# First group of a recurrent encoder layer on one core: weights in contiguous rows, two blocks per input piece, a constant as warm-up operand

## The chip, the cores and the metric

The kernel runs on one core of a Trainium2 chip. The metric is the device time of one execution in microseconds. The kernel before was timed three times. Besides, one execution was recorded by the hardware profiler; all times of single instructions are from that one.

## The reference, cut to what matters

One layer, 1024 positions by 1024 channels, all float32. The input product makes six blocks of 1024 columns; a gated linear recurrence (A) and a multi-scale pooling (B) work on two of them, the others are gates.

```python
h = x @ w_in + b_in                       # 1024 x 1024  @  1024 x 6144
xa, za, xb, zb, ga, gb = split(h)
ya = RG_LRU(causal_conv4(xa)) * silu(za)
yb = MultiScalePool(xb) * silu(zb)
y  = (sigmoid(ga) * (ya @ w_proj_a) + sigmoid(gb) * (yb @ w_proj_b)) @ w_out + b_out
out = LayerNorm(alpha * x + y)
```

## The kernel before, in words

**Products.** A float32 operand is split into a rounded high part (a CAST on ACT, names ending in h) and a low part (a TENSOR_TENSOR subtraction on DVE, names ending in l). Each product is three passes into one PSUM bank: high by high, weight high by input low, weight low by input high (`passes`, line 449). Two output blocks of 128 columns, one from each half of a section, are made together as a 2x2 block product with seven instead of eight multiplications (Winograd's form). So there are seven inputs `X[1..7]` and for every group seven weights. The names are: `x13` (products 1 and 3), `x2` and `xb` plain quarters of the input; `x57` and `x64` sums of quarters, from the raw sums `t13` and `t24`; `wa` (products 1, 2), `wb` (7, 5), `wc` (6, 3) and `wd` (4) for the weights, from the raw `ra` and `rb`. A product of one group is 12 matmuls of 512 columns: four pieces of 128 in depth, three passes each.

**Order.** PE's order is the program's. The first group, "G0" (gate columns 0 and 4), is made from plain quarters, 8 products of 4 pieces, while the input comes in (bank names `ps_s`, lines 953 to 1098). Group A0 follows (line 1125 on): product 1 (`a_A`), 2 (`e_A`), 5 (`f_A`, copied out by ACT as `m5`), 7 (`c_A`, copied out as `m7`), 3 (`f_A` again). Then it runs mixed with the next group, G1: products 1 and 2 of G1 (`a_G`, `e_G`), 6 of A0 (`a_A`), 7 of G1 (`c_G`), 6 of G1 (`a_G`), 4 of A0 (`c_A`), and so on through 24 groups, the two projections and the output product.

**The planner.** Nothing is issued directly. `Plan.add` (line 179) records every instruction with its data dependences; `Plan.order` (line 252) goes through them as a list scheduler, with a cost for each kind of instruction, a due time that follows from PE's ideal times (line 260) and the costs behind, and picks on ACT, DVE, SP and POOL the ready task that is due first, holding back when one that is due earlier becomes ready soon. `emit` writes them out in that order, so that every instruction stands at line 388. On the chip each engine then works strictly in the written order: an instruction that waits holds all that stand behind it on its engine.

**The start.** DVE clears a tile `warm` (line 955), and PE does WARM = 6 products of zeros with it. ACT issues the transfers of the first quarter of the two weight blocks (`w0r`, `dma_w0`), SP those of the input (`xr`) and the later weights. The weight block lies in HBM as 128 partitions x 8 pieces x 128 columns. A quarter of depth takes pieces q and q + 4 of it, so a transfer of one quarter has two rows of 512 bytes per partition, that of two quarters two rows of 1 KB. The first quarter of block 0 comes as two transfers of 64 KB. In the loop at line 1082 the first 512 x 128 input piece is used in two halves of 256 columns with block 0; the second piece (`kh == h == 1`) is used whole with block 0, and only then block 1 is split and used with both pieces.

**The end.** SP loads the weights of the output product (`wor`, in two transfers for each of its seven steps), the rows of the layer norm, and fills seven eighths of the output with a bias row (line 1429), to which POOL later adds.

Of the kernel before, what the change touches and what calls it, by code (L numbers as in the profile page):

```python
# [11 lines left out]
F32 = mybir.dt.float32  # L12
F32R = mybir.dt.float32r
AF = mybir.ActivationFunctionType
ALU = mybir.AluOpType

P = 128
# [3 lines left out]
H = 512  # L21
# [2 lines left out]
EPS = 1e-5  # L24
WINDOWS = (2, 4, 8, 16)
PAD = 16
WARM = 6
NW = 10
NR = 4
NWORK = 10  # L30
# [367 lines left out]


@with_exitstack  # L400
def layer_kernel(ctx: ExitStack, tc: tile.TileContext, xq, x, w_in, par, wg, w_pool, wpa, wpb, w_out, rows, out):
    nc = Plan(tc)

    def pool(name, bufs, space=None):
# [13 lines left out]
    def xt(name, dt=F32R, shape=(P, 2, H)):  # L418
        return xpool.tile(list(shape), dt, tag="x", name=name)

    def wt(name, dt=F32R, shape=(P, 2, H)):
        return wpool.tile(list(shape), dt, tag="w", name=name)
# [4 lines left out]
    def kt(name, dt=F32):  # L427
        return kpool.tile([P, S], dt, tag="k", name=name)

    def et(name):  # L430
        return epool.tile([P, H], F32, tag="e", name=name)

    def bank(name):
        return psum.tile([P, H], F32, tag="ps", name=name)
# [4 lines left out]
    out = Ref(result, as_strided(Ref.base, [S, D], [D, 1]))  # L439
    HALF = [slice(0, H), slice(H, S)]  # L440
    V, A = nc.vector, nc.scalar
# [8 lines left out]
    def split(raw, hi, lo):  # L450
        A.copy(hi, raw)
        V.tensor_tensor(lo, raw, hi.bitcast(F32), ALU.subtract)

    def passes(ps, w, m, first, last):
        (wh, wl), (mh, ml) = w, m
        for i, (a, b) in enumerate(((wh, mh), (wh, ml), (wl, mh))):
            nc.tensor.matmul(ps, a, b, start=first and i == 0, stop=last and i == 2, skip_group_check=True)
# [9 lines left out]
    KQ = 4  # L467
# [127 lines left out]
    order = [("G", 0)]  # L595
# [4 lines left out]
    def blocks_of(kind, c):  # L600
        if kind == "A":
            return XA + c, ZA + c
        if kind == "B":
            return XB + c, ZB + c
        sec = GA if c < 4 else GB
        return sec + c % 4, sec + c % 4 + 4
# [297 lines left out]
    def b_pool(g):  # L904
# [15 lines left out]
        if g == 1:  # L920
# [5 lines left out]
    sp, m, nl, y, z, z2, acc = (const.tile([P, 8], F32, name=n)  # L926
                                for n in ("sp", "sp_m", "sp_nl", "sp_y", "sp_z", "sp_z2", "sp_acc"))
# [22 lines left out]


    begin = ctx.enter_context(ExitStack())
    pass
    warm = kt("warm", F32R)[:, :H]
    V.memset(warm.bitcast(F32), 0.0)
    psw = bank("ps_warm")
    for i in range(WARM):
        nc.tensor.matmul(psw, warm[:, 0:P], warm, start=True, stop=True)
    first = blocks_of(*order[0])
    wr, wh, wl = [[f(f"{t}{n}") for n in range(2)] for t, f in  # L960
                  (("w0r", lambda n: wt(n, F32)), ("w0h", wt), ("w0l", wt))]

    xr = [[kt(f"xr{q}_{i}", F32) for i in range(2)] for q in range(KQ)]
    x13 = [[xt(f"x13{t}{q}") for t in "hl"] for q in range(KQ)]
    x2 = [xt(f"x2_{q}") for q in range(KQ)]
    xb = [xt(f"xb_{q}") for q in range(KQ)]

    def w0_part(t, n, a, b):
        return t[n].rearrange("p h (k m) -> p h k m", m=P)[:, :, a:b, :]

    def dma_w0(n, a, b, h=slice(0, 2)):

        (A if a == 0 else nc.sync).dma_start(w0_part(wr, n, a, b)[:, h], w_in[first[n]].rearrange("p (h k) m -> p h k m", h=2)[:, h, a:b, :])

    def split_w0(n, a, b, h=slice(0, 2)):
        split(*(w0_part(t, n, a, b)[:, h] for t in (wr, wh, wl)))

    def dma_x(q, i, sl=slice(0, S)):
        nc.sync.dma_start(xr[q][i][:, sl], xq[q, i][:, sl])


    def quarter(q, kh, h):
        if kh == h:
            return x13[q][0][:, kh, :], x13[q][1][:, kh, :]
        t = x2[q] if kh else xb[q]
        return t[:, 0, :], t[:, 1, :]
# [3 lines left out]
    def split_x(q, kh, h, sl=slice(0, H)):  # L990
        i, p = raws[kh, h]
        split(xr[q][i][:, HALF[p]][:, sl], *(t[:, sl] for t in quarter(q, kh, h)))

    ps0 = [[bank(f"ps_s{n}_{h}") for h in range(2)] for n in range(2)]

    def mm0(q, kh, h, n, cs=slice(0, H)):
        sl = slice(q * P, (q + 1) * P)
        passes(ps0[n][h][:, cs], (wh[n][:, kh, sl], wl[n][:, kh, sl]), tuple(t[:, cs] for t in quarter(q, kh, h)),
               q == 0 and kh == h and cs.start == 0, q == KQ - 1 and kh != h)


    PARTS = [slice(0, H // 2), slice(H // 2, H)]
    dma_w0(0, 0, 1, slice(0, 1))
    with nc.within(-2 * SOON):
        for sl in PARTS:
            dma_x(0, 0, sl)
    dma_w0(0, 0, 1, slice(1, 2))
    dma_w0(1, 0, 1)
    dma_x(0, 0, HALF[1])
    dma_x(0, 1, HALF[0])  # L1010
# [14 lines left out]
    t13, t24 = [None] * KQ, [None] * KQ  # L1025
# [15 lines left out]

    def sum57(q):
        t13[q] = xt(f"t13_{q}", F32)
        r = xr[q][0].rearrange("p (i s) -> p i s", i=2)
        V.tensor_tensor(t13[q], r, xr[q][1][:, HALF[0]].unsqueeze(1).to_broadcast((P, 2, H)), ALU.subtract)

# [19 lines left out]
    def parts(q, n=0):  # L1066
        r = xr[q][0].rearrange("p (i s) -> p i s", i=2)
        todo = [(r, *x13[q])] + [(xr[q][raws[p][0]][:, HALF[raws[p][1]]], *quarter(q, *p)) for p in ((0, 1), (1, 0))]
        for raw, t, u in todo[n:]:
            hi(raw, t)  # L1070
        for raw, t, u in todo[n:]:
            lo(raw, t, u)
        for kh, h in ((0, 0), (1, 1), (0, 1), (1, 0)):
            for n in range(2):
                mm0(q, kh, h, n)

    def each(f, qs, *a):
        for q in qs:
            f(q, *a)

    split_w0(0, 0, 1, slice(0, 1))
    for kh, h in ((0, 0), (1, 1), (0, 1), (1, 0)):
        if kh == h == 1:
            split_w0(0, 0, 1, slice(1, 2))
        for sl in PARTS if kh == h == 0 else (slice(0, H),):
            split_x(0, kh, h, sl)
            mm0(0, kh, h, 0, sl)
        if kh == h == 1:
            split_w0(1, 0, 1)
            mm0(0, 0, 0, 1)  # L1090
        if kh or h:
            mm0(0, kh, h, 1)
    for i in range(2):
        split_x(1, i, i)
        split_w0(i, 1, 2)
# [3 lines left out]
    w = weights_steps(1)  # L1099
    lower, upper = (0, 1), (2, 3)  # L1100
    each(sum57, lower)
    parts(2)
    each(hi57, lower)
    each(lo57, lower)
    parts(3)
    hi(w.ra, w.pair("wa", (1, 2))[0])
    each(sum57, upper)
    lo(w.ra, *w.tiles["wa"])
    w.sums75(wt("sb_A0", F32))
# [247 lines left out]
    for i, (n, j) in enumerate(steps):  # L1357
# [7 lines left out]
        if j == 1:  # L1365
            a, c, m1, um = [[None] * KQ for _ in range(4)]
        X_, W_ = ([(hi_[:, k, :], lo_[:, k, :]) for hi_, lo_ in ops[i][o:o + 2] for k in range(2)] for o in (0, 2))
        for g in range(KQ):
# [5 lines left out]
            for q in range(KQ):  # L1374
                sl = slice(q * P, (q + 1) * P)
# [10 lines left out]
            if (n, j) in DONE:  # L1386
                d, h = DONE[n, j]
                d += g
                if j == 3:
                    t, u = ps, et(f"c12_{n}{g}") if n == "b" else None  # L1390
                else:
                    t = u = m1[g] if j == 2 else um[g][:, HALF[h]]
# [12 lines left out]
            if (n, j, g) in CASTS:  # L1405
                k = CASTS.index((n, j, g))
# [89 lines left out]
    a, c = ([None] * KQ for _ in range(2))  # L1496
# [89 lines left out]
```

## Time and profile before

| quantity | value |
|---|---|
| median of 3 runs | 740.57 us (740.27 to 740.96) |
| profiled execution, its own time | 740.07 us |
| its span in the trace | 738.3 us |
| PE busy | 729.5 us, 99% of the span |
| DVE / ACT / POOL busy | 600.8 / 459.0 / 67.9 us |
| moved by DMA | 158.98 MB, mean 215 GB/s |

The span is from the first to the last instruction in the trace; the rest of the execution's time, 1.8 us, lies around it. PE works without a pause from the first microseconds to about 7 us before the end. In the views a row is start, duration, engine, line, operation, output <- inputs, shapes. A matmul's duration reaches to its modelled end; the step from one matmul's start to the next is what a matmul costs in the stream. The views leave out the numbers in the names: `m_A<-f_A` is `m5_A0<-f_A0`, `t<-t,xr` is a sum `t24`, `ps_s` is any of the four banks of G0.

### The profile page before, as it was taken

To read this page: it belongs to the slowest core of one execution; us is meant where nothing else is said; L and a number is where in the kernel's file an instruction comes from. 1 tells how busy PE (TensorE), PEld (TensorE's weight loads), DVE (VectorE), ACT (ScalarE), POOL (GpSimd) and SP (SyncE) were. 2 spreads that over 40 slices of the span, in tenths; PEclk is the share of its full clock that TensorE was granted. 3 is DMA by queue.
4 is the path that set the end of the run, shared out by engine and by line. 5 is a ranking of instruction groups with operands and counts; after the bars stand their busy time and mean duration, and the time that the engine had idled before them with its cause. 6 is when DMAs were issued, how large, how long until landed. Compare 5 with 4: busy or idle time off the path is not lost.

```text
span 738.3 us, 8785 instructions
## 1 busy us (share of the span) xinstructions
PE 729.5 (99%) x3249; PEld 599.4 (81%) x3249; DVE 600.8 (81%) x741; ACT 459.0 (62%) x587; POOL 67.9 (9%) x119
## 2 busy tenths in 40 slices
PE   9999999999999999999999999999999999999996
PEld 7887888888787878788888888888888888888885
DVE  7999796969696878977986768879948786999686
ACT  7686959686877868688844445447553545315473
POOL 0171011111101111100011100100000000000021
PEclk9999999999999999999999999999999999999999
DMA  9247979588988989842187954999679996758748
GB/s 320 111 142 198 264 180 279 135 240 224 303 161 217 328 206 282 219 113 91 54 204 154 212 114 158 278 315 331 235 241 303 311 333 234 267 201 232 196 80 149
DMA packets 64227, 158.98 MB, mean 215 GB/s; under 512 B 4340, under 2 KB 8308, under 8 KB 64120
## 3 DMA queue, kind: packets, MB, share of 16 engines
q1 hardware_dynamic: 43512, 106.26, 41.4%
q0 software_dynamic: 20112, 51.91, 33.6%
q8 instruction: 25, 0.41, 0.2%
q10 hardware_dynamic: 560, 0.26, 0.1%
q14 instruction: 18, 0.15, 0.1%
HBM read 137.43 MB, written 77.07 MB: 291 GB/s over the span
## 4 chain that ended last, share of the span: by engine, by line
PE 99%; DVE 1%; DVEq 0%; issue 0%
PE a_A L388 11%; PE a_B L388 11%; PE a_G L388 11%; PE oa L388 6%; PE pa_a L388 6%; PE pa_b L388 6%; PE c_B L388 6%; PE c_A L388 6%; PE c_G L388 5%; PE ps_s L388 3%; PE oc L388 3%; PE pc_b L388 3%; PE pc_a L388 3%; PE ps_pool L388 3%; PE e_B L388 3%; PE e_A L388 3%
## 5 line engine op out<-in xcount | busy, mean ns | idle before, releaser
L388 ACT ACT_TABLE_LOAD x38 | 48.8, 1283 | 3.0 <-issue 2.3
L388 DVE TENSOR_TENSOR i<-i,xc 128x1024 f32<-128x1024 f32 x8 | 9.8, 1225 | 26.9 <-ACT i L388 26.9
L388 DVE SCALAR_TENSOR_TENSOR xc<-xp,par_sb,xc 128x1023 f32<-128x1023 f32 (+2 forms) x24 | 30.7, 1281 | 0.5
L388 PE MATMUL pa_a<-oh,oh 128*128 128x512 f32 x64 | 24.9, 389 | 0.0
L388 PE MATMUL pa_a<-ol,oh 128*128 128x512 f32 x64 | 24.9, 389 | 0.0
L388 PE MATMUL pa_a<-oh,ol 128*128 128x512 f32 x64 | 24.9, 389 | 0.0
L388 PE MATMUL pa_b<-oh,oh 128*128 128x512 f32 x64 | 24.9, 389 | 0.0
L388 PE MATMUL pa_b<-ol,oh 128*128 128x512 f32 x64 | 24.9, 389 | 0.0
L388 PE MATMUL pa_b<-oh,ol 128*128 128x512 f32 x64 | 24.9, 389 | 0.0
L388 ACT ACTIVATE zb<-zb,par_sb 128x1024 f32<-128x1024 f32 (+1 forms) x16 | 15.0, 938 | 14.2 <-DVE zb L388 14.1
L388 ACT ACTIVATE r<-ps_g,par_sb 64x512 f32<-64x512 f32 x32 | 21.9, 683 | 2.1 <-DVE rb_B L388 0.8
L388 ACT ACTIVATE i<-ps_g,par_sb 64x512 f32<-64x512 f32 x32 | 21.9, 684 | 1.9 <-DVE r L388 1.4
L388 PE MATMUL c_A<-x64h,wd_A 128*128 128x512 f32 x64 | 21.0, 389 | 0.0
L388 PE MATMUL c_B<-x64h,wd_B 128*128 128x512 f32 x64 | 21.0, 389 | 0.0
L388 POOL DMA_DIRECT2D out<-y x7 | 8.5, 1210 | 130.0 <-ACT sd L388 117.4
L388 PE MATMUL ps_pool<-mixh,wp 128*128 128x512 f32 x64 | 20.3, 389 | 0.0
L388 PE MATMUL e_A<-x,wah_A 128*128 128x512 f32 x64 | 19.7, 389 | 0.0
L388 PE MATMUL e_B<-x,wah_B 128*128 128x512 f32 x64 | 19.7, 389 | 0.0
L388 POOL COPY paced<-pace 128x1 f32<-128x1 f32 x17 | 6.4, 376 | 130.9 <-ACT pace L388 130.9
L388 PE MATMUL c_G<-x64h,wd_G 128*128 128x512 f32 x56 | 18.4, 389 | 0.0
L388 DVE TENSOR_TENSOR_SCAN r<-a,i 128x1024 f32<-128x1024 f32 x8 | 18.3, 2284 | 0.1
L388 PE MATMUL e_G<-x,wah_G 128*128 128x512 f32 x56 | 17.2, 389 | 0.0
(521 smaller groups left out, 2534.5 us busy)
## 6 DMA issues: line engine op xcount, KB each, us to landing
sg<-sg SPq DMA_DIRECT2D x16, 512.0 KB, 4.3
ra_A<-in_w_in SPq DMA_DIRECT2D x8, 512.0 KB, 7.1
rb_A<-in_w_in SPq DMA_DIRECT2D x8, 512.0 KB, 7.5
xb<-bias SPq DMA_DIRECT2D x4, 1024.0 KB, 12.8
ya<-r SPq DMA_DIRECT2D x8, 512.0 KB, 5.7
xb<-in_x POOLq DMA_DIRECT2D x4, 1024.0 KB, 8.8
ra_B<-in_w_in SPq DMA_DIRECT2D x8, 512.0 KB, 4.3
rb_B<-in_w_in SPq DMA_DIRECT2D x8, 512.0 KB, 6.6
```

Of the source, the lines that this page charges most:

```text
L388: getattr(getattr(nc, t.op[0]), t.op[1])(*a, **k)
```

## The change

The host gives the two blocks of the first group once more as an array `w0`, laid out [block, partition, quarter, half, column], and the tiles `w0r`, `w0h` and `w0l` get the same layout. A quarter is then one row of 1 KB per partition, two quarters are one of 2 KB. The first quarter of each block is one transfer of 128 KB on ACT's queue (two in all where there were three). The warm-up's tile and its clearing are gone: PE multiplies a constant zero, read with step 0, WARM = 8 times. Both blocks are used on each piece of the first quarter in turn, and the second piece is also used in two halves with block 0. `sum57(0)` is done in two halves. Nothing else in the program's text changes.

```diff
-WARM = 6
+WARM = 8
...
-    warm = kt("warm", F32R)[:, :H]
-    V.memset(warm.bitcast(F32), 0.0)
+    warm = tc.nc.const_aps.tensor(0.0, [P, H]).bitcast(F32R)
...
-    wr, wh, wl = [[f(f"{t}{n}") for n in range(2)] for t, f in
-                  (("w0r", lambda n: wt(n, F32)), ("w0h", wt), ("w0l", wt))]
+    wr, wh, wl = [[wt(f"{t}{n}", dt, (P, KQ, 2, P)) for n in range(2)] for t, dt in
+                  (("w0r", F32), ("w0h", F32R), ("w0l", F32R))]
...
+    def dma_w0(n, a, b):
+        (A if a == 0 else nc.sync).dma_start(wr[n][:, a:b], w0[n][:, a:b])
+    def split_w0(n, a, b):
+        split(*(t[n][:, a:b] for t in (wr, wh, wl)))
...
-    dma_w0(0, 0, 1, slice(0, 1))
+    dma_w0(0, 0, 1)
     with nc.within(-2 * SOON):
         for sl in PARTS:
             dma_x(0, 0, sl)
-    dma_w0(0, 0, 1, slice(1, 2))
     dma_w0(1, 0, 1)
...
+        if q == 0:
+            for i in range(2):
+                V.tensor_tensor(t13[q][:, i, :], xr[q][0][:, HALF[i]], xr[q][1][:, HALF[0]], ALU.subtract)
+            return
...
-    split_w0(0, 0, 1, slice(0, 1))
     for kh, h in ((0, 0), (1, 1), (0, 1), (1, 0)):
-        if kh == h == 1:
-            split_w0(0, 0, 1, slice(1, 2))
-        for sl in PARTS if kh == h == 0 else (slice(0, H),):
-            split_x(0, kh, h, sl)
-            mm0(0, kh, h, 0, sl)
-        if kh == h == 1:
-            split_w0(1, 0, 1)
-            mm0(0, 0, 0, 1)
-        if kh or h:
-            mm0(0, kh, h, 1)
+        for n in range(2):
+            if kh == h == 0:
+                split_w0(n, 0, 1)
+            for sl in PARTS if kh == h and n == 0 else (slice(0, H),):
+                if n == 0:
+                    split_x(0, kh, h, sl)
+                mm0(0, kh, h, n, sl)
...
+        "w0": np.ascontiguousarray(w_blocks[[32, 36]].reshape(2, P, 2, 4, P).transpose(0, 1, 3, 2, 4)),
```

The planner orders the whole program anew from these tasks, so the written order also differs in places that the diff does not name. Here the rows keep the numbers in the names; the number after the last underscore only counts tiles.

ACT at the end of group A0's weights, before: `wch_A0` is the last weight of A0, `wah_G1` the first high weight of G1, `m5` and `m7` the copies of PE's products 5 and 7.

```order
L388 COPY m1_A0_370<-a_A0_347 128x512
L388 CAST wch_A0_380<-ra_A0_126 128x1024
L388 ACT_TABLE_LOAD
L388 ACTIVATE sp_y_399<-sp_m_377 128x8
L388 CAST wah_G1_401<-ra_G1_183 128x1024
L388 COPY m5_A0_430<-f_A0_392 128x512
L388 ACT_TABLE_LOAD
L388 ACTIVATE sg32_4_467<-ps_s1_0_178,par_sb_163 128x512
L388 ACTIVATE sg32_4_467<-ps_s1_1_186,par_sb_163 128x512
L388 COPY m7_A0_485<-c_A0_427 128x512
```

And ACT at the same place now.

```order
L388 COPY m1_A0_371<-a_A0_346 128x512
L388 CAST wch_A0_389<-ra_A0_125 128x1024
L388 ACT_TABLE_LOAD
L388 ACTIVATE sp_y_408<-sp_m_386 128x8
L388 COPY m5_A0_419<-f_A0_391 128x512
L388 CAST wah_G1_434<-ra_G1_193 128x1024
L388 COPY m7_A0_460<-c_A0_417 128x512
L388 ACT_TABLE_LOAD
L388 ACTIVATE sg32_4_490<-ps_s1_0_165,par_sb_170 128x512
```

`wah_G1` stood ahead of `m5_A0`, which reads a product of PE; now it stands behind it, and `m7_A0` is ahead of the gate's activations.

DVE where it makes G1's weights 7, 5, 6 and 3 (`wbl`, `wcl`), now:

```order
L388 TENSOR_TENSOR wd_G1_557<-rb_G1_236,wd_G1_557 128x512
L388 TENSOR_TENSOR rb_G1_236<-rb_G1_236 128x512
L388 TENSOR_TENSOR rb_G1_236<-ra_G1_193,rb_G1_236 128x512
L388 TENSOR_TENSOR ra_G1_193<-rb_G1_236,ra_G1_193 128x512
L388 TENSOR_TENSOR sg32_1_584<-e_G1_525,m1_G1_533 128x512
L388 TENSOR_TENSOR wbl_G1_588<-rb_G1_236,wbh_G1_581 128x1024
L388 TENSOR_TENSOR ra_G1_193<-ra_G1_193 128x512
L388 SCALAR_TENSOR_TENSOR xp0_395<-f_A0_391,par_sb_170,u2_A0_586 128x512
L388 TENSOR_TENSOR z0_605<-a_A0_346,m5_A0_419 128x512
L388 TENSOR_TENSOR wcl_G1_610<-ra_G1_193,wch_G1_601 128x1024
```

Between `wal_G1` and these rows stand the same 14 instructions of DVE as before, the sums `t24` and the low parts `x64l`; behind the second `ra_G1`, `xp0` stands where `wd_A0` stood.

PE's first rows, before:

```order
L388 MATMUL ps_warm_104<-warm_85 128x512 x6
L388 MATMUL ps_s0_0_150<-x13h0_142,w0h0_145 128x256
L388 MATMUL ps_s0_0_150<-x13l0_147,w0h0_145 128x256
L388 MATMUL ps_s0_0_150<-x13h0_142,w0l0_152 128x256
L388 MATMUL ps_s0_0_150<-x13h0_142,w0h0_145 128x256
L388 MATMUL ps_s0_0_150<-x13l0_147,w0h0_145 128x256
L388 MATMUL ps_s0_0_150<-x13h0_142,w0l0_152 128x256
L388 MATMUL ps_s0_1_168<-x13h0_142,w0h0_145 128x512
L388 MATMUL ps_s0_1_168<-x13l0_147,w0h0_145 128x512
L388 MATMUL ps_s0_1_168<-x13h0_142,w0l0_152 128x512
```

And now, `ps_s0` and `w0h0` being block 0, `ps_s1` and `w0h1` block 1:

```order
L388 MATMUL ps_warm_85<-const-float32-0.0 128x512 x8
L388 MATMUL ps_s0_0_151<-x13h0_141,w0h0_144 128x256
L388 MATMUL ps_s0_0_151<-x13l0_146,w0h0_144 128x256
L388 MATMUL ps_s0_0_151<-x13h0_141,w0l0_149 128x256
L388 MATMUL ps_s0_0_151<-x13h0_141,w0h0_144 128x256
L388 MATMUL ps_s0_0_151<-x13l0_146,w0h0_144 128x256
L388 MATMUL ps_s0_0_151<-x13h0_141,w0l0_149 128x256
L388 MATMUL ps_s1_0_165<-x13h0_141,w0h1_154 128x512
L388 MATMUL ps_s1_0_165<-x13l0_146,w0h1_154 128x512
L388 MATMUL ps_s1_0_165<-x13h0_141,w0l1_160 128x512
L388 MATMUL ps_s0_1_175<-x13h0_141,w0h0_144 128x256
```

Block 1 now comes between the two pieces of block 0. Near the end SP's row `wor3_1` (half of the output product's weights for its step 3) stands behind the two norm rows and four of the seven fills of the output, where it stood ahead of them all.

More of the change, by code (lines that the diff above doesn't have):

```diff
@@ L400, in layer_kernel @@
 @with_exitstack
-def layer_kernel(ctx: ExitStack, tc: tile.TileContext, xq, x, w_in, par, wg, w_pool, wpa, wpb, w_out, rows, out):
+def layer_kernel(ctx: ExitStack, tc: tile.TileContext, xq, x, w0, w_in, par, wg, w_pool, wpa, wpb, w_out, rows, out):
     nc = Plan(tc)
@@ L952, in layer_kernel @@
     begin = ctx.enter_context(ExitStack())
-    pass
-    warm = kt("warm", F32R)[:, :H]
-    V.memset(warm.bitcast(F32), 0.0)
+    warm = tc.nc.const_aps.tensor(0.0, [P, H]).bitcast(F32R)
     psw = bank("ps_warm")
@@ L958, in layer_kernel @@
         nc.tensor.matmul(psw, warm[:, 0:P], warm, start=True, stop=True)
-    first = blocks_of(*order[0])
-    wr, wh, wl = [[f(f"{t}{n}") for n in range(2)] for t, f in
-                  (("w0r", lambda n: wt(n, F32)), ("w0h", wt), ("w0l", wt))]
+    wr, wh, wl = [[wt(f"{t}{n}", dt, (P, KQ, 2, P)) for n in range(2)] for t, dt in
+                  (("w0r", F32), ("w0h", F32R), ("w0l", F32R))]
     xr = [[kt(f"xr{q}_{i}", F32) for i in range(2)] for q in range(KQ)]
@@ L966, in layer_kernel @@
     xb = [xt(f"xb_{q}") for q in range(KQ)]
[L968 to L976, printed above, removed]
+    def dma_w0(n, a, b):
+        (A if a == 0 else nc.sync).dma_start(wr[n][:, a:b], w0[n][:, a:b])
+    def split_w0(n, a, b):
+        split(*(t[n][:, a:b] for t in (wr, wh, wl)))
     def dma_x(q, i, sl=slice(0, S)):
@@ L996, in mm0 @@
     def mm0(q, kh, h, n, cs=slice(0, H)):
-        sl = slice(q * P, (q + 1) * P)
-        passes(ps0[n][h][:, cs], (wh[n][:, kh, sl], wl[n][:, kh, sl]), tuple(t[:, cs] for t in quarter(q, kh, h)),
+        passes(ps0[n][h][:, cs], (wh[n][:, q, kh, :], wl[n][:, q, kh, :]), tuple(t[:, cs] for t in quarter(q, kh, h)),
                q == 0 and kh == h and cs.start == 0, q == KQ - 1 and kh != h)
     PARTS = [slice(0, H // 2), slice(H // 2, H)]
-    dma_w0(0, 0, 1, slice(0, 1))
+    dma_w0(0, 0, 1)
     with nc.within(-2 * SOON):
@@ L1562 @@
     rows = np.stack([np.asarray(b_out[0]), np.asarray(ln_gain[0]), np.asarray(ln_bias[0])])
+    w_blocks = blocks(w_in[0])
     xt = x2.T.reshape(2, 4, P, 2, H)
@@ L1568 @@
         "x": np.ascontiguousarray(x2),
-        "w_in": blocks(w_in[0]),
+        "w0": np.ascontiguousarray(w_blocks[[32, 36]].reshape(2, P, 2, 4, P).transpose(0, 1, 3, 2, 4)),
+        "w_in": w_blocks,
         "par": par,
```

## The prediction

> **What bounds the kernel now.** I read the page's shares and its chain first, then PE's waits, then the two stretches which the change touches. The page's first part and the chain that ended last:
>
> ```profile
> PE 729.5 (99%) x3249; PEld 599.4 (81%) x3249; DVE 600.8 (81%) x741; ACT 459.0 (62%) x587; POOL 67.9 (9%) x119
> PE 99%; DVE 1%; DVEq 0%; issue 0%
> ```
>
> PE is the chain. The view of the waits, asked for PE between 9 and 731 us, answers with its heading and no row:
>
> ```profile
> core 0 of [0], span 738.3 us
> engine line waited for: us in total, times, longest us
> ```
>
> So PE never waits there, and the time is: when PE reaches its steady step, plus a fixed stream of matmuls, plus the tail. A change can win only at the start, and it loses wherever another engine now delivers later than PE asks. PE's timeline at the start:
>
> ```profile
> 1.44 2.93 PE L388 MATMUL ps_warm<-warm 128*128 128x512 f32 x6 [1.44 <-DVE warm L388]
> 4.38 0.58 PE L388 MATMUL ps_s<-x13h,w0h 128*128 128x256 f32 x1
> 4.77 0.46 PE L388 MATMUL ps_s<-x13l,w0h 128*128 128x256 f32 x1
> 5.45 0.41 PE L388 MATMUL ps_s<-x13l,w0h 128*128 128x256 f32 x1
> 5.67 0.41 PE L388 MATMUL ps_s<-x13h,w0l 128*128 128x256 f32 x1
> 7.07 0.63 PE L388 MATMUL ps_s<-x13h,w0l 128*128 128x512 f32 x1
> 7.49 0.44 PE L388 MATMUL ps_s<-x13h,w0h 128*128 128x512 f32 x1
> 8.70 0.39 PE L388 MATMUL ps_s<-x13h,w0l 128*128 128x512 f32 x1
> 8.93 0.39 PE L388 MATMUL ps_s<-xb,w0h 128*128 128x512 f32 x1
> ```
>
> Until 7.49 a matmul of 512 columns costs 0.42 us (7.07 to 7.49) and one of 256 columns 0.22 (5.45 to 5.67); from about 7.5 on one of 512 costs 0.23 (8.70 to 8.93). PE's speed doubles once, some 6.1 us after its first matmul at 1.44. At 8.93 the first input quarter is through with both blocks on both pieces: 12 units of 512 columns. I compare the kernels at this point.
>
> **The start, part by part.** What ACT and DVE feed there:
>
> ```profile
> 0.90 0.48 DVE L388 MEMSET warm<- 128x512 f32 x1 [0.90 <-PEq L1578]
> 3.73 0.41 ACT L388 CAST x13h<-xr 128x256 fp32r<-128x256 f32 x1
> 4.04 0.29 ACT L388 CAST w0h<-w0r 128x128 fp32r<-128x128 f32 x1
> 5.60 0.40 ACT L388 CAST w0h<-w0r 128x256 fp32r<-128x256 f32 x1
> 6.34 0.42 DVE L388 TENSOR_TENSOR w0l<-w0r,w0h 128x256 fp32r<-128x256 f32 x1
> 7.81 0.69 DVE L388 TENSOR_TENSOR xb<-xr,xb 128x512 fp32r<-128x512 f32 x1
> ```
>
> Warm-up: the memset and the wait for it go, so PE starts about where DVE started, at 0.90, 0.54 earlier. Eight warm-up matmuls are six of 2.93 and two of 0.42 more, and end near 4.6 with the last one's tail; their cover is the wait for the data, and without it they would cost 0.2.
>
> Weights: the first piece is now 128 KB in 1 KB rows, like the first input piece, which was issued at the same moment and was cast at 3.73. So I expect it there about 0.1 later than the old 64 KB. Its cast takes 0.40 instead of 0.29, so the first real matmul starts near 4.65 instead of 4.38. That costs nothing later: block 1's first quarter no longer queues third (its low half ended at 6.76, 6.34 + 0.42; now near 5.7, being the second of two transfers and the fourth cast).
>
> PE's sum, if its speed still doubled at 7.5: six matmuls of 256 (0.39 and five of 0.22) bring 4.65 to 6.1, three of 512 (1.27) to 7.4: six units by 7.4 where the trace has six by 7.49. The other six then end near 8.83: a gain of 0.1. If the doubling follows the first matmul, 0.54 earlier, half of these 0.54 is gained on top: 0.35 in all. If the doubling came before 4.7, the data would bound: block 1's low half at 5.7, the piece's second halves to 6.4, then the rest at 0.23 a unit, 12 units by 7.76: a gain of 1.17. I take 0.35, as the one that moves with what the row shows (PE's own first matmul); 0.1 and 1.17 are the ends. The next data, `xb`, were complete at 8.50 (7.81 + 0.69) beside 8.93, and DVE's half-size sum now lets them through some 0.9 earlier, so nothing is late there. The halved sum and the three more, smaller matmuls together cost under 0.1, in cover.
>
> **The planner's new order, ACT and DVE at 34 to 53 us.** This I hold to be the larger part. PE there:
>
> ```profile
> 35.91 0.39 PE L388 MATMUL f_A<-x57h,wbl_A 128*128 128x512 f32 x1
> 49.73 0.39 PE L388 MATMUL c_G<-x57h,wbh_G 128*128 128x512 f32 x1
> 50.19 0.39 PE L388 MATMUL c_G<-x57h,wbl_G 128*128 128x512 f32 x1
> 52.45 0.39 PE L388 MATMUL a_G<-x64h,wch_G 128*128 128x512 f32 x1
> 52.91 0.39 PE L388 MATMUL a_G<-x64h,wcl_G 128*128 128x512 f32 x1
> ```
>
> Product 5 of A0 ends at E = 36.30 (35.91 + 0.39). PE asks for `wbh_G` at E + 13.43, for `wbl_G` at E + 13.89, and, with step 0.2267 (ten matmuls from 50.19 to 52.45), for `wch_G` and `wcl_G` ten and twelve matmuls later. These distances belong to PE and do not change. ACT and DVE deliver:
>
> ```profile
> 34.04 1.04 ACT L388 CAST wah_G<-ra_G 128x1024 fp32r<-128x1024 f32 x1
> 36.33 0.59 ACT L388 COPY m_A<-f_A 128x512 f32<-128x512 f32 x1 [1.25 <-PE f_A L388]
> 46.97 1.05 ACT L388 CAST wbh_G<-rb_G 128x1024 fp32r<-128x1024 f32 x1 [0.62 <-DVE rb_G L388]
> 50.03 1.05 ACT L388 CAST wch_G<-ra_G 128x1024 fp32r<-128x1024 f32 x1 [0.87 <-DVE ra_G L388]
> 35.12 1.24 DVE L388 TENSOR_TENSOR wal_G<-ra_G,wah_G 128x1024 fp32r<-128x1024 f32 x1 [0.41 <-ACT wah_G L388]
> 36.27 4.31 DVE L388 SCALAR_TENSOR_TENSOR t<-t,xr 128x512 f32<-128x512 f32 x7
> 45.46 0.69 DVE L388 TENSOR_TENSOR rb_G<-rb_G 128x512 f32<-128x512 f32 x1
> 46.19 0.69 DVE L388 TENSOR_TENSOR rb_G<-ra_G,rb_G 128x512 f32<-128x512 f32 x1
> 47.53 0.68 DVE L388 TENSOR_TENSOR sg<-e_G,m_G 128x512 f32<-128x512 f32 x1
> 48.13 1.22 DVE L388 TENSOR_TENSOR wbl_G<-rb_G,wbh_G 128x1024 fp32r<-128x1024 f32 x1
> 49.26 0.69 DVE L388 TENSOR_TENSOR ra_G<-ra_G 128x512 f32<-128x512 f32 x1
> 51.12 1.23 DVE L388 TENSOR_TENSOR wcl_G<-ra_G,wch_G 128x1024 fp32r<-128x1024 f32 x1
> ```
>
> Before, `wah_G` (34.04) was done ahead of the copy `m5`, which ACT can start only when PE has ended product 5 (36.33, after 1.25 idle). Now the copy stands first, and `wah_G` waits behind it on ACT, `wal_G` on DVE for `wah_G`, and behind `wal_G` all sums for G1. Step by step, from E: copy at +0.03; `wah_G` follows one copy later, at +0.5 (0.59 less an overlap of 0.1), to +1.55; `wal_G` from +1.6; the sums `t` start 1.15 after it (35.12 to 36.27), at +2.75. Before they started at 36.27, E - 0.03: DVE is 2.8 later. From the first `t` to the first `rb_G` are 15 instructions back to back, 9.19 us (36.27 to 45.46), with no idle time in their rows, so nothing there takes up the delay: first `rb_G` at +11.95, the second 0.73 later and 0.69 long, done at +13.37. `wbh_G` runs from +13.4 to +14.45.
>
> PE asks at +13.43 and gets it at about +14.5: a stall of 1.06. `wbl_G` comes behind the sum `ra_G` and `sg` on DVE: start +14.62, end +15.85; PE's third matmul stands ready at +14.95 and starts at +15.88: 0.93. The last sum `ra_G` ends at +16.45 (1.13 and 0.69 after `wbl_G`'s start), `wch_G` at +17.58, `wcl_G` (1.23) at +18.85; PE, ten matmuls after +15.88, wants `wch_G` at +18.15, which is there, and `wcl_G` at +18.60: 0.28. Sum 2.27. Before, the same three were ready at 48.02, 49.35 and 52.35 and had 1.7, 0.8 and 0.6 to spare. Bounds: with 0.60 for each of the 15 and nothing for signals 1.8; with 0.1 more at each of the five hand-overs between engines 2.6. It does not depend on the start, since all is counted from E.
>
> SP's row `wor3_1` now stands behind six other transfers:
>
> ```profile
> 668.96 6.06 SPq L388 DMA_DIRECT2D out<-in_rows  x7
> 685.72 1.05 ACT L388 CAST wo3h<-wor 128x1024 fp32r<-128x1024 f32 x1 [6.97 <-PE oc L388]
> ```
>
> It is issued at the latest when the seven fills were, by 675.0, and is first read at 685.7: nothing, in the cover of these 10 us; gone, each microsecond late would be one on ACT. The other exchanged rows I cost at 0, bounds -0.1 and +0.5.
>
> **Sum.** -0.35 + 2.27 = +1.92 on the profiled execution's 740.07 gives 742.0. The median of the runs, 740.57, is 0.5 above that execution; on the median it is 742.5.
>
> **The rivals.** *The early clock (not slower).* If PE's speed doubles before 4.7 us, the start gains 1.17: -1.17 + 2.27 = +1.1, 741.7; with the stalls' low end of 1.8, 741.2. That is within 0.2% (1.48 us, about what a measurement of this kernel can tell from no change). It decides below a doubling at about 5.0. For it: PE now is at work from 0.9 without the pause at 4.2, and one doubling at 7.5 does not tell what started its clock. Against it: six warm-up matmuls, 2.9 us of work, did not bring it about before. [...] Chance 0.2.
>
> *No stall at `c_G`.* The delay of 2.8 is absorbed, or the copy is not waited for: only -0.35 is left, 740.2. It decides if `wbh_G` starts by E + 12.4. For it: ACT and DVE each idle in this stretch. Against it: those idle times lie ahead of E, and the 15 instructions behind have none. Chance 0.07.
>
> *More stalls.* ACT and DVE run 2.3 later against SP's and POOL's work, and the next groups' weights come late too: one more stall like the second, 0.9, makes 743.4. The spare 0.6 to 1.7 above shows how little is needed; against it, the whole stream has moved by the same amount as PE. Chance 0.08.
>
> **How the numbers follow.** The forecast has 0.65. 742.5 is its time; its own range, from gains of 0.1 to 0.6 and stalls of 1.8 to 2.6, is 741.8 to 743.1. Down to 741.2 the early clock is in; up to 743.3, which takes in a small further stall. Left out are the case without stalls and the upper part of the last. Slower by over 0.2% is above 742.05: most of the forecast (0.57) and the last rival (0.08), 0.65. Within 0.2%: the early clock, a small part of the forecast, the case without stalls, 0.33. Faster by over 0.2% needs a gain of 1.48, more than the start holds: 0.02.
>
> **What would show it.** In the trace after: PE's first matmul near 0.9, the first real one near 4.65, the step of 0.23 reached near 7, `xb` near 8.6. On ACT `m_A<-f_A` ahead of `wah_G`; DVE idle some 2 us before `wal_G`; PE waiting for ACT `wbh_G` and DVE `wbl_G` near 50, 2 us together. Wrong: no PE wait there; a step of 0.23 from the first real matmul on; or a PE wait that this text does not name.

## The result, and the profile after

The kernel after took 743.51 us (median of 6 runs, 742.40 to 745.03), the kernel before beside it 740.62 (6 runs, 740.27 to 740.96): a ratio of 1.004, 95% interval 1.0027 to 1.0053. That is 2.89 slower; 742.5 was forecast, and 743.51 lies above the range. The profiled execution of after took 742.40, 2.33 more than that of before. So there are two things to explain: 2.33 in the profile, and 1.1 between the profile and the median.

The view of PE's waits between 9 and 731 us had no row before. Of after:

```profile
core 0 of [0], span 740.6 us
engine line waited for: us in total, times, longest us
PE c_G L388 <- ACT wbh_G L388: 1.0, 1, 1.0
PE c_G L388 <- DVE wbl_G L388: 0.6, 1, 0.6
```

They stand where the prediction put them. PE's timeline of after, the start and these waits:

```profile
0.77 3.67 PE L388 MATMUL ps_warm<-const-float32-0.0 128*128 128x512 f32 x8 [0.77 <-PEq L1571]
4.82 0.39 PE L388 MATMUL ps_s<-x13h,w0h 128*128 128x256 f32 x1 [0.39 <-ACT w0h L388]
8.66 0.72 PE L388 MATMUL ps_s<-xb,w0h 128*128 128x512 f32 x2
27.82 0.39 PE L388 MATMUL a_A<-x13h,wah_A 128*128 128x512 f32 x1
49.36 0.39 PE L388 MATMUL a_A<-x64h,wcl_A 128*128 128x512 f32 x1
50.70 0.50 PE L388 MATMUL c_G<-x57h,wbh_G 128*128 128x512 f32 x1 [0.95 <-ACT wbh_G L388]
51.03 0.40 PE L388 MATMUL c_G<-x57l,wbh_G 128*128 128x512 f32 x1
52.02 0.50 PE L388 MATMUL c_G<-x57h,wbl_G 128*128 128x512 f32 x1 [0.59 <-DVE wbl_G L388]
52.36 0.40 PE L388 MATMUL c_G<-x57h,wbh_G 128*128 128x512 f32 x1
54.67 0.39 PE L388 MATMUL a_G<-x64l,wch_G 128*128 128x512 f32 x1
55.03 0.50 PE L388 MATMUL a_G<-x64h,wcl_G 128*128 128x512 f32 x1
55.37 0.40 PE L388 MATMUL a_G<-x64h,wch_G 128*128 128x512 f32 x1
```

What a start-to-start distance has over the steady 0.228 is lost: 1.11 at 49.36, 0.11 and 0.76 around 51, 0.11 at 52.02, 0.13 and 0.11 at 55: 2.33 together. The view of waits names only the two large ones. The start has 0.27 less at the first `xb` matmul (8.66 against 8.93), 0.15 less at the first matmul of group A0 (27.82 against 27.97).

From here on each profile is read by three numbers: A, the start of the first `a_A` matmul (27.97 before); W, what PE loses between A and 60 us, summed as above; and the rest of the execution's time. The rest hardly moves: 740.07 - 27.97 = 712.10 before, 742.40 - 27.82 - 2.33 = 712.25 after, and 712.06 to 712.28 in 16 of the 18 profiles told here. The other two, of the kernels with six rows put back, lose another 0.3 near 81 us.

### The profile page after: what moved, and what is told of

Read it like the earlier page. It is cut to its first block, busy times and chain, and to the rows that moved or that the text cites. A ratio compares the mean times of both kernels' runs of the same rounds, so it can differ in the third digit from the quotient of the medians.

```text
span 740.6 us, 8797 instructions
## 1 busy us (share of the span) xinstructions
PE 730.4 (99%) x3254; PEld 599.1 (81%) x3254; DVE 600.9 (81%) x741; ACT 459.2 (62%) x587; POOL 67.5 (9%) x119
## 4 chain that ended last, share of the span: by engine, by line
PE 96%; DVE 2%; DMA 1%; issue 0%; ACT 0%; DVEq 0%; SPq 0%
PE a_B L388 11%; PE a_A L388 11%; PE a_G L388 10%; PE oa L388 6%; PE pa_b L388 6%; PE pa_a L388 6%; PE c_B L388 6%; PE c_A L388 6%; PE c_G L388 5%; PE ps_s L388 3%; PE oc L388 3%; PE pc_b L388 3%; PE pc_a L388 3%; PE ps_pool L388 3%; PE e_B L388 3%; PE e_A L388 3%
```

## The experiments

The planner's rows were put back one by one, with a helper that moves one task next to another on its engine and keeps all data dependences; the other engines' rows stay word for word. `put(order, engine, task, other)` puts a task ahead of another one, with a fifth number ahead of a later one of that name, with a sixth behind it. The diffs below are shortened to what matters. The kernels ran in four sets on different chips; before was timed in each of them, and its medians agree within 0.12, so kernels of different sets are compared below.

| kernel | median us (runs), range | profiled us | A | W |
|---|---|---|---|---|
| before, in four sets | 740.72 to 740.84 (21 to 30), 739.47 to 742.37 | 740.07 | 27.97 | 0.00 |
| after, first set | 743.51 (6), 742.40 to 745.03 | 742.40 | 27.82 | 2.33 |
| after, again | 742.13 (7), 742.05 to 743.59 | 742.12 | 27.53 | 2.33 |
| after, cast first | 742.04 (11), 741.82 to 743.82 | 741.82 | 27.41 | 2.28 |
| after, two back | 742.00 (11), 741.87 to 743.83 | 742.06 | 27.57 | 2.21 |
| after, three back | 741.82 (11), 741.72 to 743.77 | 741.82 | 27.50 | 2.05 |
| after, four back | 740.31 (11), 740.22 to 742.25 | 741.94 | 29.19 | 0.59 |
| after, six back | 740.64 (11), 740.23 to 741.94 | 740.43 | 27.67 | 0.26 |
| before, copy first | 743.43 (5), 743.28 to 744.40 | 743.39 | 28.95 | 2.34 |
| before, constant warm-up | 740.68 (11), 740.13 to 741.20 | 740.24 | 28.18 | 0.00 |

**Cast first.** One row of after is put back, the one that the prediction named:

```diff
-        order = self.order()
+        order = self.ahead(self.order(), "wah_G1", "m5_A0")
```

> The kernel after, with one instruction put back: on ACT the cast wah_G of group G1 stands ahead of the copy m5 of product 5 again. Theory S (stall, then clock): the exchanged row costs 2.2 to 2.3 us of PE waits at 49 to 55 us, and since PE then idles about 2 us within a few us, some runs get half the granted clock for one more stretch, which is the 1.1 us by which the median of after lies above its profiled run. Then here both go: median 740.4 (before less the 0.15 to 0.27 which the start gained), all runs within about 0.7 us, mean clock of each 0.998. Theory D (the start): the waits cost their 2.3 in every run, but the extra 1.1 comes from the start, where PE is idle for data between 4.4 and 6.5 us after its clock has come early. Then here only 2.3 goes: median 741.2, runs still 2 us apart, some mean clocks at 0.996.

Measured 742.04, ratio 1.002 (1.0012 to 1.0029), and in the profile the waits had not gone:

```profile
PE c_G L388 <- ACT wbh_G L388: 0.9, 1, 0.9
PE c_G L388 <- DVE wbl_G L388: 0.6, 1, 0.6
```

Both theories had taken for granted that they would go. DVE of this kernel shows what took the place of the late cast:

```profile
36.37 1.29 DVE L388 SCALAR_TENSOR_TENSOR t<-t,xr 128x512 f32<-128x512 f32 x2
39.11 0.69 DVE L388 TENSOR_TENSOR m_A<-m_A,m_A 128x512 f32<-128x512 f32 x1 [1.45 <-ACT m_A L388]
```

`wal_G` and the first sums are early again, but after two sums instead of seven DVE comes to `m_A`, the sum of the copies of products 5 and 7, and stands still until PE has ended product 7 and ACT has copied it. That row too had been exchanged: between `wal_G1` and `wd_G1` stand the same 14 instructions as before, as said ahead of the prediction, but not in the same order. In after the row does not wait (40.11), since DVE is late there anyway, after idling 1.98 for `wah_G` ahead of `wal_G` (37.75).

**Copy first, in before.** A first kernel moves the copy and not the cast:

```diff
-        order = self.order()
+        order = self.ahead(self.order(), "m5_A0", "wah_G1")
```

> The kernel before, with the one exchange alone: on ACT the copy m5 of product 5 stands ahead of the cast wah_G of group G1. Start as before. Both theories: PE waits for wbh_G near 50 us, for wbl_G 0.3 us later and for wcl_G near 55, 2.2 to 2.4 us together. Theory S (stall, then clock): the median is more than that above before, 743.3 to 744, runs 1 to 2 us apart, some mean clocks 0.996. Theory D (the start): 742.9, runs within 0.7 us, clock 0.998.

Measured 741.71 (11 runs, 741.15 to 742.11), no wait at `c_G`; PE waits 0.7 for the copy at `f_A` instead. But this is not the exchange: the copy now precedes most of product 5 in the program, and takes it after four of its twelve matmuls (at 35.63, with `f_A` begun at 34.52), so the last eight are missing from it. It says nothing about the question. A second kernel moves the cast behind the copy:

```diff
-        order = self.order()
+        order = self.put(self.order(), "ACT", "wah_G1", "m5_A0", 0, 1)
```

> The kernel before with one exchange alone, the whole product in the copy this time: on ACT m5 stands ahead of wah_G, all else in before's order. By the prediction's step the first t starts 2.8 us later than before, and PE waits for wbh_G 1.06, wbl_G 0.93, wcl_G 0.28: 2.27, so 743.0. Rival: ACT and DVE catch up (ACT's table load and sg no longer have to wait, x64h run ahead of x64l), a third of the delay is absorbed: 741.5 to 742.3.

Measured 743.43 against 740.79, ratio 1.0042 (1.0029 to 1.0054). ACT's rows and PE's waits of this kernel:

```profile
37.30 0.59 ACT L388 COPY m_A<-f_A 128x512 f32<-128x512 f32 x1 [2.39 <-PE f_A L388]
37.79 1.05 ACT L388 CAST wah_G<-ra_G 128x1024 fp32r<-128x1024 f32 x1
```

```profile
PE c_G L388 <- ACT wbh_G L388: 0.9, 1, 0.9
PE c_G L388 <- DVE wbl_G L388: 0.6, 1, 0.6
PE ps_s L388 <- DVE xb L388: 0.3, 1, 0.3
```

The exchange alone does in before what the prediction worked out: W is 2.34, 2.27 was forecast. Nothing was absorbed. The third row belongs to the start, which came late in this execution (more below).

**Two, three, four and six rows back, in after.** The line of three back; two back leaves out the move of `m7_A0`, four back adds `"ACT", "m1_G1", "wd_G1", 0, 1`, six back besides that `"ACT", "wch_G1", "u2_A0"` and `"DVE", "wcl_G1", "xp0", 1`:

```diff
-        order = self.order()
+        order = self.put(self.put(self.put(self.order(), "ACT", "wah_G1", "m5_A0"), "ACT", "m7_A0", "bias"), "DVE", "m5_A0", "t24_", 7)
```

> As the run before it in this set, but with the copy m7 left ahead of the table load on ACT; wah_G and DVE's sum m_A are back in before's places. Theory T: ACT waits for product 7 until 38.5, and so table load, sg and the casts x64h stand as late as in the kernel after (x64h from 42.6); DVE's x64l then wait for x64h instead, and its first rb_G comes at 47.0 to 47.5: PE waits of 1.5 to 2.2 us are left, 741.2 to 741.9. If ACT's place of m7 does not matter: no wait, 739.7.

("The run before it" is three back.)

With two back (742.00, ratio 1.0024, 1.0015 to 1.0033) DVE does its eight sums in one piece, and then:

```profile
43.38 3.34 DVE L388 TENSOR_TENSOR x64l<-t,x64h 128x512 fp32r<-128x512 f32 x5 [1.33 <-ACT x64h L388]
```

ACT waits for product 7 ahead of its table load, so the casts `x64h` are late and DVE waits for them. W is 2.21, at the upper end of what was expected.

> The kernel after with three of its exchanged rows put back where before has them: on ACT the cast wah_G ahead of the copy m5, on ACT the copy m7 (m_A<-c_A) behind the two sg instead of ahead of the table load, on DVE the sum m_A behind seven sums t instead of two. Theory T (three exchanges, each enough by itself): with one put back the waits at 49 to 55 us stayed at 2.27, because DVE then waited 1.45 us for the copy m7; with all three back no PE wait is left near 50 us, and the time is that of the first run less 2.3: 739.7, below before. Theory O (another cause, say a transfer or the weights' sums themselves): the waits stay, 742.

With three back (741.82, ratio 1.0022, 1.0013 to 1.0031) the waits were still there, against theory T as it was written. ACT and then DVE of this kernel:

```profile
44.06 0.59 ACT L388 COPY m_G<-a_G 128x512 f32<-128x512 f32 x1 [1.98 <-issue]
```

```profile
45.20 1.30 DVE L388 TENSOR_TENSOR x64l<-t,x64h 128x512 fp32r<-128x512 f32 x2 [1.40 <-ACT x64h L388]
```

A fourth copy, of G1's product 1, stands ahead of casts `x64h` that DVE needs, and ACT idles 1.98 us ahead of it. The view names no releaser; PE's last matmul of that product ends at 43.98, and the copy starts at 44.06.

> The kernel after with four exchanged rows in before's places: the three of the run with three put back, and besides on ACT the copy m_G of product 1 of G1, which stood ahead of two casts x64h and both wd and waited 1.98 us for PE there; now it stands behind wd_G again. Theory T (a chain of copies, each waiting for its product ahead of the weights' work): now DVE's x64l are done by 45.1, rb_G starts near 45.8, wbh_G near 47.2, PE asks near 49.3: no wait of PE near 50, time as the three put back less 2.1: 739.7, below before's 740.8. Theory O (something else delays DVE): waits of over 1 us stay, 741 or more.

With four back the waits at `c_G` are gone. Of 0.59 one wait is left in the view:

```profile
PE a_G L388 <- DVE wcl_G L388: 0.3, 1, 0.3
```

Six of the eleven runs took 740.22 to 740.31, 1.5 below the eight shorter ones of three back (741.72 to 741.88); the median of 740.31 stands against 740.84 of before, ratio 1.0004 (0.9995 to 1.0012), no difference. The first `rb_G`, counted from A, comes at 17.5 in before (45.46), at 20.3 in after (48.09), at 20.1 and 20.0 with two and three back (47.71 and 47.49), at 17.9 with four (47.10, with A late at 29.19).

> The kernel after with four exchanged rows put back as before, and two more: on ACT the cast wch_G ahead of the copy u_A, on DVE wcl_G ahead of the sum xp that waits for u_A. Theory T (copies that wait for products, ahead of the weights' work): the last wait, 0.6 us at wcl_G near 54 us, goes; no PE wait is left, main group of runs 739.6 to 739.8 (740.27 less 0.6), 1.0 below before. If wcl_G is late for another reason: 740.3 as with four.

With six back the view of PE's waits has no row, W is 0.26, but about 0.3 came up near 81 us in their place, and the median is 740.64 against 740.78, ratio 1.0001 (0.9992 to 1.0010). Five of its runs, 741.07 to 741.94, are above 741; the shortest of all, 740.23, is not below those of four back. The forecast 739.7 was not reached.

**The start.** Two kernels change the warm-up alone. In before, with all rows kept:

```diff
+    warm.tile.real = tc.nc.const_aps.tensor(0.0, [P, S]).bitcast(F32R)   # besides, the clearing is left out and 2 of the 6 matmuls are written twice
```

> The kernel before, with the warm-up alone changed: eight matmuls on the constant in place of six on a tile that DVE clears; all else in before's order. Both theories: PE's first matmul near 0.8 instead of 1.44, the first real one at 4.4 as before since the data bound it. Theory S: the clock is granted up to one stretch earlier, gain 0.1 to 0.6 us, no wider spread, median 740.0 to 740.5. Theory D: PE waits for data at an early clock, runs spread over 2 us, median 740.6 or above, some mean clocks 0.996.

Measured 740.68 against 740.72, ratio 1.0001 (0.9992 to 1.0010), runs 740.13 to 741.20: no difference that can be told; the median fits what theory D expected, the spread what theory S did. And after with the cast first and before's warm-up:

```diff
-    warm = tc.nc.const_aps.tensor(0.0, [P, H]).bitcast(F32R)   # 8 matmuls
+    warm = kt("warm", F32R)[:, :H]   # cleared by DVE, 6 matmuls
```

> The kernel after with wah_G ahead of m5 as in the first run of this set, and with before's warm-up (DVE clears a tile, six matmuls on it); weights in rows of 1 and 2 KB, both blocks on each piece, first sum in halves stay. What is left of the change is the data path of the start. If that path helps by itself as the prediction had it (first quarter's second block no longer third in the queue): 740.5. If the larger weight rows take their time from the input pieces, as after's later casts of x13h (4.06 and 5.28 against 3.73 and 4.31) say: 740.9 to 741.3, first xb matmul at 9.0 to 9.4.

Measured 742.07 (8 runs, 741.87 to 743.62) against 742.04 with the constant: no difference again. But the expectation of 740.5 to 741.3 had counted on the waits being gone. The last of this kind is four back with before's order of the first units:

```diff
-            for sl in PARTS if kh == h and n == 0 else (slice(0, H),):
+        for sl in PARTS if kh == h == 0 else (slice(0, H),):   # block 0 on both pieces, then block 1
```

> The run before it in this set, but with before's order of the first units: block 0 on both pieces, then block 1 (and the second piece cast whole). Weights in rows of 1 and 2 KB in two transfers and the constant warm-up stay. If the gain at the start is the layout's (block 1's first quarter no longer is the third transfer in ACT's queue, which was cast at 6.6 to 7.5 in three of four profiles of before's start): as the run before it within 0.3. If it is the order of the units (PE has both blocks' work on the first piece while the second is under way): 0.5 to 1.0 longer.

Measured 741.52 (11 runs, 740.41 to 742.19). Its W is 0.00 where four back has 0.59; its five shortest runs, 740.41 to 740.56, have A near 28.3 (less 712.2), the six of four back near 27.5 (740.27 less 712.2 less 0.59, if W is that of its profile). By this the order of the units would carry about 0.8 of the gain at the start, weights and halved sum about 0.3 of the 1.1 against before's 28.6 (740.72 less 712.1). That is an estimate from the shorter runs alone, with a W taken from one profile each; it is not shown.

Why before's A is nearer to 28.6 than to the 27.97 of its profile, ACT's timeline shows: the cast of block 1's first weights stood at 5.60 there, and waited for nothing. In three more profiles of the same data path (the two kernels with the copy first, and that with the constant) it is:

```profile
7.47 0.40 ACT L388 CAST w0h<-w0r 128x256 fp32r<-128x256 f32 x1 [1.77 <-DMA w0r<-in_w_in]
```

```profile
7.33 0.40 ACT L388 CAST w0h<-w0r 128x256 fp32r<-128x256 f32 x1 [1.60 <-DMA w0r<-in_w_in]
```

```profile
6.57 0.41 ACT L388 CAST w0h<-w0r 128x256 fp32r<-128x256 f32 x1 [0.81 <-DMA w0r<-in_w_in]
```

The cast has to wait for the third transfer in the queue and comes up to 1.9 later, and A is 29.08, 28.95 and 28.18: 21.6 behind this cast in all three, so here the data set the start. By that, a cast at 5.60 would have given 27.2. Before's profiled execution was lucky in its transfer, and lost part of it again to a late clock: PE's full step came near 7.5 there, and its matmuls of 256 columns up to 5.67 take 0.41, where in the first kernel with the copy first, with the same warm-up, such a matmul takes 0.28 at 5.07. In after the same cast stands at 5.59, and waits for nothing, but the second input piece ahead of it comes later than before (4.31):

```profile
5.28 0.41 ACT L388 CAST x13h<-xr 128x256 fp32r<-128x256 f32 x1 [0.51 <-DMA xr<-in_xq]
5.59 0.40 ACT L388 CAST w0h<-w0r 128x256 fp32r<-128x256 f32 x1
```

**The two groups of times.** After was run again, and single executions of it were profiled three more times:

> The kernel after once more, to see its spread beside the others on one chip. If the 1.1 us by which the median lay above the profiled run belongs to the kernel (its start or its waits under another phase of the clock): median 743.0 to 743.6, runs 1.5 us or more apart. If it belonged to those few runs: as in the first run of the earlier set, where ten of eleven lay within 0.4 us: 742.2 to 742.6.

> The kernel after, one look, to catch in a profile the upper of its two groups of times (742.1 and 743.3 to 743.6). If a run near 743.5 comes: theory G (the clock at the start comes one stretch of 3.4 us later, near 8 to 9 us) has the first xb matmul near 9.8 and the waits at 50 us unchanged; theory H (the clock is halved for a stretch after the waits at 50 us) has the first xb near 8.5 and matmuls of 0.43 us somewhere behind.

> The same look once more, for the same reason: near 743.5 theory G has a first xb matmul near 9.8, theory H a stretch of matmuls of 0.43 us behind 50 us; near 742.1 neither.

> The kernel after, one look for a run of its upper group. Near 743.5 or above, theory G has the full clock late (near 9) or withdrawn for one stretch of 3.4 us near 8, as in the profile of the run without the new order of units; near 742.1 the full clock by 6 us and no break.

The second set gave 742.13, ratio 1.0025 (1.0014 to 1.0035), the single executions 742.25, 742.35 and 743.98. With the first set these are 16 runs in two groups: eight of 742.05 to 742.40, with mean clocks of 0.997 and 0.998, and eight of 743.26 to 745.03, all with 0.995 or 0.996. One stretch of 3.41 us at half the clock takes 3.41 / 2 / 742 = 0.0023 from the mean. The execution of 743.98 shows one. Its windows, cut where the granted clock changes (52.54 and 55.95) and 3.41 apart on both sides of it (PE alone: length, busy us and matmuls, granted clock, DMA share, GB/s):

```profile
core 0: us, PE busy (x), PEclk, DMA share, GB/s
45.72:49.13 3.41, 3.41 (x17) 1.00 0.49 192
49.13:52.54 3.41, 1.86 (x8) 1.00 0.00 0
52.54:55.95 3.41, 3.41 (x9) 0.50 0.51 150
55.95:59.36 3.41, 3.41 (x16) 1.00 0.83 299
```

In 49.13 to 52.54 PE stands still for the waits (0.95 and 0.60) and is busy 1.86 of 3.41; for the next 3.41 us the granted clock is 0.50. PE's timeline has eight steps of 0.43 there (52.32 to 55.74):

```profile
52.32 0.63 PE L388 MATMUL c_G<-x57h,wbl_G 128*128 128x512 f32 x1 [0.60 <-DVE wbl_G L388]
52.75 0.63 PE L388 MATMUL c_G<-x57h,wbh_G 128*128 128x512 f32 x1
...
55.31 0.63 PE L388 MATMUL c_G<-x57h,wbh_G 128*128 128x512 f32 x1
55.74 0.50 PE L388 MATMUL c_G<-x57l,wbh_G 128*128 128x512 f32 x1
```

W is 3.68 instead of 2.33, 1.35 more, which takes in that the wait at `wcl_G` falls away while PE is slow; A is 28.12, and 743.98 - 28.12 - 3.68 = 712.18. This run's excess is accounted for, and theory H (S in the first set) holds for it. The trace of after has the granted clock full from 4.22 to 738.09, 733.87 long, that of before from 7.58 to 734.62, 727.04 long: 6.83 apart, and 215 and 213 times 3.4133. On this grid, counted back from 738.09, the same waits lie in one stretch of after too, PE is busy for as little, and the clock stays:

```profile
core 0: us, PE busy (x), PEclk, DMA share, GB/s
48.59:52.01 3.42, 1.89 (x8) 1.00 0.00 0
52.01:55.42 3.41, 3.40 (x14) 1.00 0.48 156
```

The 0.03 between 1.86 and 1.89 are nothing to go by: with the stretch begun at 49.12 the first is 1.88. In nine other profiles stretches near 50 us with 1.96 to 2.83 busy kept the full clock. What decides is not seen in these rows. That the other seven runs of the upper group are of the same kind rests on their times (five of them, 743.26 to 743.59, lie 1.2 above the eight of the lower group, about the price worked out here) and on their mean clocks. The second sign is weak: 0.996 is also in the profile of cast first, which took 741.82 and has the full clock from 45 to 59 us, and a stretch lost at the start, as shown next, lowers the mean just as much (0.994). Before with the copy first, which has the same waits, has two of five runs at 744.01 and 744.40 with 0.996 and 0.995.

There is a second loss of time to the clock, at the start. The profile of four back is one of that kernel's four longer runs (741.94): PE's timeline,

```profile
7.55 0.63 PE L388 MATMUL ps_s<-x13h,w0l 128*128 128x512 f32 x1
9.26 0.56 PE L388 MATMUL ps_s<-x13h,w0h 128*128 128x512 f32 x1
9.65 0.40 PE L388 MATMUL ps_s<-x13l,w0h 128*128 128x512 f32 x1
29.19 0.39 PE L388 MATMUL a_A<-x13h,wah_A 128*128 128x512 f32 x1
```

takes 0.43 from one start to the next at 7.55, has the full step (0.24) only from 9.65 on, and A is 29.19. The profile of cast first with the old warm-up is one of that kernel's longer runs as well (743.23, where six of its eight took 741.87 to 742.48), with W 2.18 and A 28.84:

```profile
7.20 0.63 PE L388 MATMUL ps_s<-x13l,w0h 128*128 128x512 f32 x1
7.62 0.63 PE L388 MATMUL ps_s<-x13h,w0l 128*128 128x512 f32 x1
9.11 0.40 PE L388 MATMUL ps_s<-x13h,w0h 128*128 128x512 f32 x1
9.35 0.39 PE L388 MATMUL ps_s<-x13l,w0h 128*128 128x512 f32 x1
```

Its mean clock is 0.999, that of four back's profile 0.998: the mean does not show a full clock that comes late. And in the profile of four back with the old order of units (742.19) the full clock comes, is withdrawn for one stretch, and comes again; the windows of this kernel, all engines:

```profile
core 0: us, PE busy (x) PEld busy (x) DVE busy (x) ACT busy (x) POOL busy (x), PEclk, DMA share, GB/s
4.43:7.84 3.41, 2.71 (x10) 1.57 (x10) 2.69 (x6) 2.29 (x6) 0.00 (x0) 1.00 0.96 357
7.84:11.26 3.42, 3.42 (x10) 2.64 (x9) 3.34 (x7) 2.47 (x6) 0.00 (x0) 0.50 0.99 365
11.26:14.67 3.41, 3.41 (x17) 2.80 (x16) 3.41 (x6) 3.38 (x5) 0.00 (x0) 1.00 1.05 411
```

Here 2.71 busy of 3.41 was followed by half the clock, with A at 30.01. Whether work for PE in the gaps of the start helps is asked of six back and of after, with three more warm-up matmuls behind the first, third and fourth real one:

```diff
+        pe = [t for t in order if t.eng == "PE"]
+        order = [u for t in order for u in ((t, pe[0]) if t in (pe[8], pe[10], pe[11]) else (t,))]
```

> The run before it in this set, with three more warm-up matmuls (the constant, 512 columns, about 0.43 us each at the lower clock and 0.23 at the full one): behind the first, the third and the fourth real matmul, where PE waits for data. Theory G (in the upper group of runs the clock comes late, near 9 us, or is withdrawn for 3.4 us near 8 us, because PE idles between 4.4 and 6.5): the upper group goes, the full clock comes by 7.7 in every profile and stays; main group as the run before it or 0.3 above. If the upper group has nothing to do with PE's idle time at the start: 2 to 4 of 11 runs stay 1.5 to 2 us above the others.

> The kernel after, with the same three extra matmuls at the start and nothing else changed; the waits at 49 to 55 us stay. Theory G: all runs 741.9 to 742.5, none in the group at 743.3 to 745. Theory H (the waits at 50 us cost the clock): the upper group stays.

Six back with them took 740.51 (11 runs, 740.34 to 742.22), one run above 741 instead of five; its profile has A at 28.39. After with them took 742.98 (7 runs, 742.44 to 744.34): the shorter runs are 0.3 to 0.4 longer than without, and three of seven stay above 743.3, two of these with mean clocks of 0.995 and 0.996. So theory G, that the upper group of after is made at the start, falls as the only cause; for the longer runs of six back it stays possible, on five and one runs out of eleven, and not more than that.

## Why the prediction was wrong

The step that failed is the sum: "-0.35 + 2.27 = +1.92", to which the 0.5 between before's median and its profiled execution was added as a constant. It has no term for a granted clock lost behind the stall, 1.35 in the one run that shows it; by their times and mean clocks it was paid by most runs of the first set, and so it set the median. Its start is too small by half or more, and the 0.5 doesn't carry over; these two err the other way. Point by point:

**The stall's price was right, its place too.** 2.27 was forecast, 1.06, 0.93 and 0.28; 2.33 was measured, 1.22, 0.87 and 0.24 (each with the 0.11 that the step behind a wait has too much), and 2.34 with the exchange alone in before. It showed as PE waits for `wbh_G` and `wbl_G`, as announced. (The step of 0.2267 is that of twelve matmuls from 49.73 to 52.45; the ten named there give 0.226, which changes nothing in the sum.)

**Its cause was told too narrowly.** The prediction made one row responsible and costed the other exchanged rows at 0. In after, four rows do the same thing: copies of products (m5, m7, m1 of G1) and a sum that needs two of them stand ahead of work for the next weights, on engines that took their rows in order here (DVE stood still 1.45 for the copy `m7`, ACT 1.98 ahead of the copy of G1's product 1). Two of them are shown to be nearly enough by themselves, m5's exchange in before (2.34) and the copy of G1's product 1 as the last of the four in after (2.05); the other two were not tried alone. They lie side by side in time, so they cost together what one costs alone, and the sum was right by that, by luck and not by its reason; who puts one, two or three rows back has 0.05, 0.12 and 0.28 of W back in all, and with the fourth 1.74.

**The stall's second price was missing.** In one profile of after a stretch at half the clock follows directly behind the waits, and W is 1.35 more. Half of the 16 runs seem to be of this kind, by their times and mean clocks. How long PE stood still does not tell such a run from the others: with waits of 0.95 and 0.60 us and 1.86 busy of 3.41 half the clock followed in one run, while 1.89 passed in another. Without a clock lost there the time of after would be that of the lower group, 742.1. Five of the six runs that made the 743.51 were in the upper group, and so the median left the range; two of the second set's seven were, and its 742.13 lies inside. Which of the two a set of few runs shows is chance as far as is known.

**The start gained more than 0.35, and it was hidden twice.** Against the profiled execution of before A gained 0.15 (27.82 against 27.97); the eight other profiles of after's start with the full clock by about 6 us lie between 27.41 and 28.12, seven of them at a gain of 0.2 to 0.56. But that execution's third transfer came early; against before's A near 28.6, worked out from its median, these seven gain some 0.8 to 1.2. The 0.5 between before's profile and its median fits such a late transfer in most runs, which the change takes away: adding it to the forecast was wrong. Without it and with 0.4 for A and W at 2.33 the sum is 740.07 - 0.4 + 2.3 = 742.0, and the second set's 742.13 is that.

**The rival of the early clock** came true in its condition: in the profile of after PE runs 512 columns in 0.24 from the first such matmul on (6.54 to 6.78). The list of signs has this as one of being wrong, and it holds but for the first six matmuls, of 256 columns, which wait for data. The gain of 1.17 did not come against the profile, since the second input piece was cast at 5.28 instead of 4.31 and PE waited for data. Of the points that were to show it, PE's first matmul (0.77), the first `xb` (8.66), DVE's idle time ahead of `wal_G` (1.98) and the waits came out; the first real matmul at 4.82 was 0.17 late, the late transfer of the input piece was not foreseen.

**The other rivals.** "No stall" did not come. "More stalls" has 743.4, near the 743.51, but that would be luck: the view of the waits has no third row, and what lengthened the runs was another thing.

**The warm-up** was given 0.25 of the 0.35, since the full clock was to follow PE's first matmul. Alone it changes nothing that can be measured, though the interval of 0.9992 to 1.0010 (some 0.6 to 0.7 us either way) is too wide to exclude 0.25. Its reason did not hold: with the first matmul at 1.44 or 1.45, the full clock was there at 5.07 in one profile (256 columns in 0.28), near 7.5 in another, and near 9 in a third.

## What to carry to other kernels

Where a planner's order changes, look for every row on an in-order engine that now waits for a product ahead of work for the next one; several such rows hide each other, and here the time moved only when the fourth was back. A stall of the engine that bounds the kernel can cost more than its waits: here they cost 2.33 us in one profile and 3.68 in that of a run in which the granted clock fell to 0.50 behind them. And a single profiled execution has a start of its own: take the spread of its first transfers from several profiles before its distance to the median is carried over to a changed kernel.

## What was not expected of the hardware

The granted clock fell to 0.50 for exactly one stretch of 3.41 us after a stretch with PE busy 1.86 (at 49 us) or 2.71 (at 4.4 us), and came back for the next. Both stretches have that length (7.84 to 11.26, 52.54 to 55.95). When the full step first came differed by 3 us or more: of two kernels whose PE began at 0.77, both with waits for data between 4.5 and 6.5, one (after) ran 512 columns in 0.24 from 6.54 on, and one (four back) only from 9.65 on.

The third transfer of ACT's queue, 128 KB in 512-byte rows, was there for a cast at 5.60 in one execution and at 7.33 and 7.47 in others with the same start.

Still open: why a stretch with PE busy 1.86 cost the clock in one run and one with 1.89 did not in another; and whether all longer runs of the other kernels are late clocks at the start. The latter fits the seven of cast first, two and three back (743.61 to 743.83, mean clock 0.997, 1.7 to 1.9 above the others; four back's late clock cost 1.7 against an A of 27.5), but only three longer runs of kernels other than after have a profile: two with a clock that comes late (four back, and cast first with the old warm-up), one with a clock that is withdrawn.
